# Stick-breaking heads taken two at a time, and five small pads in SBUF

## The chip, the cores and the metric

One NeuronCore of a Trainium2 chip runs the whole program. The metric is the device time of one execution in microseconds. Of the kernel before, three executions took 3411.0, 3412.67 and 3414.54 us; a fourth was taken with the hardware profiler.

## The reference, cut to what matters

The reference is a chain of three transformer-like blocks on 512 tokens of 1024 channels in float32: an HGRN2 mixer, a Mamba-2 mixer and two convolutional feed-forwards; then a block with two attentions side by side; then a third block with latent attention, a convolution and a SwiGLU feed-forward. The part that the change rewrites is the stick-breaking attention of the second block, 8 heads of 64 channels:

```python
def stick_breaking_attention(q, k, v):
    # A[t,s] = beta[t,s] * prod_{s<j<t}(1-beta[t,j]), s<t
    z = einsum('bhqd,bshd->bhqs', qblk, k) * scale
    causal = kpos[None, :] < qpos[:, None]
    log_beta = log_sigmoid(z)
    log_1mb = where(causal, log_sigmoid(-z), 0.0)
    suffix = cumsum(log_1mb, axis=3, reverse=True) - log_1mb
    a = where(causal, exp(log_beta + suffix), 0.0)
    return einsum('bhqs,bshd->bqhd', a, v)
```

Beside it runs a sliding-window attention of 8 heads. Both results go through projections of their own (`w_up_a` for the stick heads, `w_up_b` for the window heads), are gated, summed and projected by `w_o`.

## The kernel before, in words

**Dense products.** Nearly all of the work is x times a weight matrix. Every float32 operand is split into a rounded part and a rest, both of type float32r (`split`, line 241: ScalarE copies the rounded part, VectorE subtracts). One block of 128 by 128 weights times 512 tokens is then three matmuls, lines 188 to 190 in `accumulate`: high weight by high x, high weight by low x, low weight by high x. The weights are the stationary operand and are split in the pool `wp` (tiles `whi`, `wlo`, three buffers each, line 165 on); the moving operand is a tile of 128 partitions by 512 float32, 2048 bytes in each partition. The x of a projection (`xh`, `xl`) lies in the pool `res`. Other moving operands lie in pools of the stage: `hh`, `hl` (hidden units of four feed-forwards, in pools `ffn`, `ffn`, `ffr` and `swi`), `ogh`, `ogl` in `hg`, `yh`, `yl` in `mb`, `oah`, `oal`, `obh`, `obl` in `at_c`, `mh`, `ml` in `at_g`, and in the third block `qah`, `kvh`, `krh`, `ph`, `at` and `mg` in its `t3` pools and `pe`.

**Where a tile lies.** Pools lie in SBUF one behind the other in the order in which they are opened, and the tiles of a pool in the order of their first use. `const`, `res`, `wp` and `tp` are opened once, in this order (lines 99 to 102); every pool of a stage lies behind `tp`. `hg` lies behind the small pool `hg_c`, `mb` behind `mb_c`, `swi` behind `xout`, and `t3_x`, `pe`, `t3_q` and `t3_h` behind `t3_k`, while `t3_g` lies where `t3_k` was, once that is closed.

**The attention stage** (`attention2`, line 1116). Its 29 projection products (`v0 v1 q0 k0 g g w1 ...`, line 1186 on) stand in a list `fill`, and the loop of line 1207 writes the program in turns: in each turn every live attention head does one step, and one projection product is taken from the list. One window head is live at a time (four steps, `window_steps`), and up to two stick heads, started at least three turns apart (`gap`, line 1221). A stick head (`stick_steps`, line 1349) does six steps: for query block i = 3, 2, 1, 0 the scores q.k of (i + 1) * 128 keys (line 1368), two sigmoids on ScalarE, two triangular selects on GpSimd, the transposes of the block before (line 1359) with their copies, and on VectorE a reversed product scan (line 1382) and a product (line 1386); then the last transposes; then the product with v (line 1393). The head's 64 channels lie in partitions 0 to 63 or 64 to 127, so line 1368 contracts over 64 rows, half of TensorE's array, and line 1393 makes 64 columns, the other kind of half. Both have plain float32 operands, and each such matmul runs as two passes. After the loop come `gated(w_up_b, ob)` and `gated(w_up_a, oa)`, lines 1253 and 1254, 96 matmuls each.

**What sets the order.** The program's order is a priority: the framework that builds the kernel orders the instructions of each engine ahead of time, and takes a later instruction earlier where its operands are ready. On the chip each engine then goes through its list in order. Worked through by hand, the loop of line 1207 takes 32 turns, with a product from `fill` in turns 0 to 27.

The start of a head in the loop, and the scores and the product with v of a head:

```python
if sticks and n < 2 and ("k", 0) in have and (n == 0 or tick >= gap):
    h = sticks.pop(0)
    while ("k", h // 2) not in have:
        fill.pop()()
...
    nc.tensor.matmul(ps[:, :w], q[:, i * P : w], k[:, :w], start=True, stop=True)
...
    nc.tensor.matmul(
        po[dst, j * P :], va[j][:, 64 * h : 64 * h + 64], at[:, at0[j] : at0[j] + NT - j * P], start=j == 0, stop=j == 3,
    )
```

Of the kernel before, what the change touches and what calls it, by code (L numbers as in the profile page):

```python
# [8 lines left out]
F32 = mybir.dt.float32  # L9
# [3 lines left out]
AF = mybir.ActivationFunctionType  # L13
ALU = mybir.AluOpType
AX = mybir.AxisListType
PSUM = bass.MemoryType.PSUM
P = 128
# [18 lines left out]
def flat_rows(ap):  # L36
    names = "abcd"[: len(ap.shape)]
    f = ap.rearrange(f"{' '.join(names)} -> ({' '.join(names)})") if len(ap.shape) > 1 else ap
    return f.rearrange("(r c) -> r c", c=P)


def view(t, off, dims):

    return bass.AP(t.tensor, t.offset + off, [t.ap[0], *dims])
# [49 lines left out]
class Net:  # L94
    def __init__(self, ctx, tc, ins):
        self.ctx, self.tc, self.nc, self.I = ctx, tc, tc.nc, ins
        self.n = 0
        pool = lambda name, bufs, **kw: ctx.enter_context(tc.tile_pool(name=name, bufs=bufs, **kw))
        self.const = pool("const", 1)
        self.res = pool("res", 1)  # L100
        self.wp = pool("wp", 2)
        self.tp = pool("tp", 2)
        self.mm = pool("mm", 4, space=PSUM)
        self.aux = pool("aux", 4, space=PSUM)
        nc = self.nc
        self.ident = self.const.tile([P, P], F32, tag="ident", name="ident")
        make_identity(nc, self.ident)
        self.ones = self.const.tile([P, P], F32, tag="ones", name="ones")
        nc.gpsimd.memset(self.ones, 1.0)
        self.zero = self.const.tile([P, 1], F32, tag="zero", name="zero")  # L110
        nc.gpsimd.memset(self.zero, 0.0)
        self.mhalf = self.const.tile([P, 16], F32, tag="mhalf", name="mhalf")
        nc.gpsimd.memset(self.mhalf, -0.5)
        self.xT = [self.res.tile([P, NT], F32, tag=f"x{j}", name=f"x{j}") for j in range(DT)]
        self.xh = self.xl = None
        self.early = []
        self.rows = self.load_rows()
# [335 lines left out]
    def hgrn2(self, nxt):  # L453
# [4 lines left out]
        with ExitStack() as st:  # L458
            pool = lambda name, bufs: st.enter_context(tc.tile_pool(name=name, bufs=bufs, reuse_waits="tile"))
            hc, hp = pool("hg_c", 1), pool("hg", 2)  # L460
            masks = hc.tile([P, 8, P], U8, tag="masks", name="hg_masks")
            for half in range(2):
                mf = self.tmp("t", bufs=5)
# [231 lines left out]
    def mamba(self, nxt):  # L695
# [6 lines left out]
        with ExitStack() as st:  # L702
            pool = lambda name, bufs, **kw: st.enter_context(tc.tile_pool(name=name, bufs=bufs, **kw))
            mc, mp = pool("mb_c", 1), pool("mb", 2)
            dram = pool("mb_d", 1, space=bass.MemoryType.DRAM)


# [408 lines left out]
    def attention2(self, nxt):  # L1116
# [5 lines left out]
        with ExitStack() as st:  # L1122
# [8 lines left out]
            with ExitStack() as st2:  # L1131
# [69 lines left out]
                fill = fill[::-1]  # L1201
                do_wq(0)
                wins = [(i, e) for i in range(4) for e in range(2)]
                sticks = list(range(8))
                live = {}
                tick = 0
                while wins or sticks or live:
                    if wins and not any(n[0] == "w" for n in live):
# [2 lines left out]
                            fill.pop()()  # L1211
                        hs = slice(64 * e, 64 * e + 64)
                        live["w", i, e] = self.window_steps(wp_, have["wq", i][hs], kb[hs], vb, e, sink, ob, 4 * e + i)
                    n = sum(n[0] == "s" for n in live)
                    if sticks and n < 2 and ("k", 0) in have and (n == 0 or tick >= gap):
                        h = sticks.pop(0)
                        while ("k", h // 2) not in have:
                            fill.pop()()
                        hs = slice(64 * (h % 2), 64 * (h % 2) + 64)
                        live["s", h] = self.stick_steps(sp, have["q", h // 2][hs], have["k", h // 2][hs], va, h, oa)  # L1220
                        gap = tick + 3
                    for name in list(live):
                        if next(live[name], "end") == "end":
                            del live[name]
# [121 lines left out]
        hi, lo = ob[h // 2]  # L1346
        self.split(hi[dst], lo[dst], po[dst])

    def stick_steps(self, pool, q, k, va, h, oa):

        nc = self.nc
        dst = slice(64 * (h % 2), 64 * (h % 2) + 64)
        at = pool.tile([P, 10 * P], F32, tag="sat", name=self.nm("sat"), bufs=2)
        at0 = [0, 4 * P, 7 * P, 9 * P]

        def turn(be, i):
            ps = self.psum("aux")
            for j in range(i + 1):
                nc.tensor.transpose(ps[:, j * P : (j + 1) * P], be[:, j * P : (j + 1) * P], self.ident)
            for j in range(i + 1):  # L1360
                to = at0[j] + (i - j) * P
                nc.scalar.activation(at[:, to : to + P], ps[:, j * P : (j + 1) * P], AF.Copy)

        last = None
        for i in (3, 2, 1, 0):
            w = (i + 1) * P
            ps = self.psum("aux")
            nc.tensor.matmul(ps[:, :w], q[:, i * P : w], k[:, :w], start=True, stop=True)  # L1368
            be = pool.tile([P, NT], F32, tag="be", name=self.nm("be"), bufs=3)
            om = pool.tile([P, NT], F32, tag="om", name=self.nm("om"), bufs=2)  # L1370
            nc.scalar.activation(om[:, :w], ps[:, :w], AF.Sigmoid, scale=-1.0)
            nc.scalar.activation(be[:, :w], ps[:, :w], AF.Sigmoid)
            for t, to in ((om, 1.0), (be, 0.0)):
                nc.gpsimd.affine_select(
                    out=t[:, i * P : w], in_=t[:, i * P : w], pattern=[[-1, P]], compare_op=ALU.is_gt, fill=to,
                    base=0, channel_multiplier=1,
                )
            if last:
                turn(*last)
            sc = pool.tile([P, NT], F32, tag="sc", name=self.nm("sc"), bufs=1)  # L1380
            nc.vector.memset(sc[:, w - 1 : w], 1.0)
            nc.vector.tensor_tensor_scan(
                out=view(sc, w - 2, [(-1, w - 1)]), data0=view(om, w - 1, [(-1, w - 1)]),
                data1=view(self.zero, 0, [(0, w - 1)]), initial=1.0, op0=ALU.mult, op1=ALU.add,
            )
            nc.vector.tensor_tensor(out=be[:, :w], in0=be[:, :w], in1=sc[:, :w], op=ALU.mult)
            last = (be, i)
            yield
        turn(*last)
        yield  # L1390
        po = self.psum("aux")
        for j in range(4):
            nc.tensor.matmul(
                po[dst, j * P :], va[j][:, 64 * h : 64 * h + 64], at[:, at0[j] : at0[j] + NT - j * P], start=j == 0, stop=j == 3,
            )
        hi, lo = oa[h // 2]
        self.split(hi[dst], lo[dst], po[dst])

    def relu_ffn(self, nxt, beside):

# [219 lines left out]
    def third(self, before):  # L1620
# [7 lines left out]
        with ExitStack() as st:  # L1628
# [9 lines left out]
            with ExitStack() as s2:  # L1638
# [7 lines left out]
                kr = tuple(kp.tile([P, NK], F32R, tag=f"kr{x}", name=f"kr{x}") for x in "hl")  # L1646
                rk = kp.tile([P, NK], F32, tag="rk", name="rk")
                rkc = kp.tile([P, 6], F32, tag="rkc", name="rkc")
                sqk = rk

                def latent(dst, ps, n, at, gain, sq, first):
# [368 lines left out]
    def swiglu(self, dst):  # L2020
# [6 lines left out]
        with ExitStack() as st:  # L2027
            pool = lambda name, bufs: st.enter_context(self.tc.tile_pool(name=name, bufs=bufs, reuse_waits="tile"))
            xp, fp = pool("xout", 1), pool("swi", 2)
            xo = [xp.tile([P, D], F32, tag=f"xo{c}", name=f"xo{c}") for c in range(4)]  # L2030

            NP = 2
# [143 lines left out]
```

## Time and profile before

| | us |
|---|---|
| median of three executions | 3412.67 |
| the profiled execution, its own time | 3415.03 |
| its span, first to last instruction | 3413.3 |
| TensorE matmul busy (PE) | 3342.7, 98% |
| TensorE weight load busy (PEld) | 2755.6, 81% |
| VectorE busy (DVE) | 2254.0, 66% |
| ScalarE busy (ACT) | 1464.2, 43% |
| GpSimd busy (POOL) | 69.2, 2% |

The profiled execution is 2.36 us over the median, and 1.7 us of it lie outside the span. Matmuls are pipelined: a 128x512 one is shown as some 0.39 us long, while the next one starts after 0.23 us. So the cost of a stream of matmuls is read from the starts, not from the durations.

### The profile page before, as it was taken

The numbers are of one execution on the slowest core, as the hardware profiler recorded it, in microseconds if no ns is written. First come the engines' busy times: TensorE is split into PE (matmuls) and PEld (weight loads), VectorE is DVE, ScalarE is ACT, GpSimd is POOL, SyncE is SP. The second block draws the span as 40 slices with busy tenths as digits, with TensorE's granted clock in tenths as the row PEclk, the third lists the DMA queues.
The fourth block names the chain that finished last, engine by engine and source line by source line (L and its number), as shares of the span: only waits on it lengthen the run. The fifth ranks groups of instructions, "written<-read, shape, count | busy, mean of one in ns | idle before, by whom it ended". The sixth has DMA issues, their size and how long they took to land.

```text
span 3413.3 us, 42607 instructions
## 1 busy us (share of the span) xinstructions
PE 3342.7 (98%) x16365; PEld 2755.6 (81%) x16365; DVE 2254.0 (66%) x3509; ACT 1464.2 (43%) x2505; POOL 69.2 (2%) x110
## 2 busy tenths in 40 slices
PE   8999999997999999999999999999999999999998
PEld 6888788886888887888877778888778888888887
DVE  5777756467888777465655587664669889654334
ACT  4344433234655554232455533333546666332223
POOL 0000000000000000000001100000000000000000
PEclk9999999998999999999999999999999999999999
DMA  4222233233444432333332265552333223423232
GB/s 118 79 63 62 63 99 97 95 93 78 129 117 117 133 112 81 99 94 98 92 87 78 89 193 172 177 170 93 100 87 87 85 76 106 139 87 99 94 98 74
DMA packets 409962, 350.43 MB, mean 103 GB/s; under 512 B 33704, under 2 KB 373407, under 8 KB 409759
## 3 DMA queue, kind: packets, MB, share of 16 engines
q1 hardware_dynamic: 405173, 345.42, 33.3%
q8 instruction: 129, 2.11, 0.3%
q10 hardware_dynamic: 4586, 2.29, 0.2%
q14 instruction: 74, 0.61, 0.1%
HBM read 333.75 MB, written 12.86 MB: 102 GB/s over the span
## 4 chain that ended last, share of the span: by engine, by line
PE 81%; DVE 3%; ACT 1%; DMA 1%; issue 1%; POOL 0%; SPq 0%; ACTq 0%; POOLq 0%; DVEq 0%
PE mm L188 23%; PE mm L190 22%; PE mm L189 22%; PE aux L1043 2%; PE aux L1980 2%; PE aux L2013 1%; PE aux L315 1%; PE aux L1368 1%; PE aux L2004 1%; PE aux L1010 1%; PE mm L1595 1%; PE aux L1065 1%; PE mm L1596 1%; PE mm L1597 1%; DVE wlo L243 1%
## 5 line engine op out<-in xcount | busy, mean ns | idle before, releaser
L188 PE MATMUL mm<-xh,whi 128*128 128x512 f32 x2584 | 1024.5, 396 | 3.4 <-ACT whi L242 2.0
L189 PE MATMUL mm<-xl,whi 128*128 128x512 f32 x2584 | 1013.4, 392 | 6.8 <-DVE xl L243 4.9
L190 PE MATMUL mm<-xh,wlo 128*128 128x512 f32 x2584 | 1011.9, 392 | 6.4 <-DVE wlo L243 6.3
L242 ACT ACTIVATE whi<-raw 128x1024 fp32r<-128x1024 f32 (+3 forms) x532 | 541.9, 1020 | 1087.0 <-PE mm L189 834.8
L243 DVE TENSOR_TENSOR wlo<-raw,whi 128x1024 fp32r<-128x1024 f32 (+3 forms) x532 | 625.1, 1176 | 509.4 <-ACT whi L242 501.1
L188 PEld LDWEIGHTS mm<-xh,whi 128*128 128x128 f32 x2584 | 487.3, 189 | 115.5 <-issue 12.3
L190 PEld LDWEIGHTS mm<-xh,wlo 128*128 128x128 f32 x2584 | 486.9, 188 | 111.3 <-DVE wlo L243 8.8
L189 PEld LDWEIGHTS mm<-xl,whi 128*128 128x128 f32 x2584 | 487.3, 189 | 108.0 <-DVE xl L243 5.2
L188 PE MATMUL mm<-hh,whi 128*128 128x512 f32 x784 | 309.5, 395 | 0.0
L190 PE MATMUL mm<-hh,wlo 128*128 128x512 f32 x784 | 308.7, 394 | 0.0
L189 PE MATMUL mm<-hl,whi 128*128 128x512 f32 x784 | 308.0, 393 | 0.0
L1916 DVE SCALAR_TENSOR_TENSOR cv<-cu,taps,cv 128x511 f32<-128x511 f32 (+14 forms) x240 | 178.1, 742 | 4.4 <-ACT cv L1912 0.7
L190 PEld LDWEIGHTS mm<-hh,wlo 128*128 128x128 f32 x784 | 146.8, 187 | 35.7
L189 PEld LDWEIGHTS mm<-hl,whi 128*128 128x128 f32 x784 | 146.8, 187 | 35.1
L188 PEld LDWEIGHTS mm<-hh,whi 128*128 128x128 f32 x784 | 146.9, 187 | 34.5
L393 DVE TENSOR_TENSOR x<-x,mm 128x512 f32<-128x512 f32 x136 | 93.1, 686 | 99.3 <-PE mm L190 99.2
L960 ACT ACTIVATE w<-w,mb_cum 128x128 f32<-128x128 f32 x256 | 80.9, 393 | 73.0 <-DMA w<-mb_rows 66.6
L242 ACT ACTIVATE hh<-t 128x512 fp32r<-128x512 f32 x98 | 61.4, 627 | 87.3 <-DVE t L430 57.5
L243 DVE TENSOR_TENSOR hl<-t,hh 128x512 fp32r<-128x512 f32 x98 | 67.6, 690 | 42.0 <-ACT hh L242 41.8
L737 DVE SCALAR_TENSOR_TENSOR cy<-mm,cols,cy 128x510 f32<-128x510 f32 (+1 forms) x112 | 83.4, 746 | 2.2 <-ACT cy L733 1.6
L1509 DVE SCALAR_TENSOR_TENSOR acc<-wm,silu_c,acc 128x512 f32<-128x512 f32 x112 | 81.1, 750 | 4.7 <-DMA wm<-in_w_mod_dram 3.3
L1043 PEld LDWEIGHTS aux<-w,xd 128*64 128x64 f32 x512 | 54.9, 137 | 12.2 <-issue 5.3
(517 smaller groups left out, 4672.5 us busy)
## 6 DMA issues: line engine op xcount, KB each, us to landing
raw<-in_ffn_w_in_dram SPq DMA_DIRECT2D x88, 512.0 KB
raw<-in_w_in_dram SPq DMA_DIRECT2D x69, 512.0 KB
raw<-in_w_ff_dram SPq DMA_DIRECT2D x64, 512.0 KB
raw<-in_w_dram SPq DMA_DIRECT2D x64, 512.0 KB
raw<-in_b_w_in_dram SPq DMA_DIRECT2D x48, 512.0 KB
wm<-in_w_mod_dram SPq DMA_DIRECT2D x48, 512.0 KB
raw<-in_a_w_in_dram SPq DMA_DIRECT2D x40, 512.0 KB
raw<-in_ffn_w_out_dram SPq DMA_DIRECT2D x40, 512.0 KB
```

The source lines that it names most:

```text
L188: nc.tensor.matmul(ps, hi[:, k, ms], xh, start=a + k == 0, stop=False)
L189: nc.tensor.matmul(ps, hi[:, k, ms], xl, start=False, stop=False)
L190: nc.tensor.matmul(ps, lo[:, k, ms], xh, start=False, stop=a + k == len(xs) - 1)
L242: self.nc.scalar.activation(hi, src, AF.Copy)
L243: self.nc.vector.tensor_tensor(out=lo, in0=src, in1=hi.bitcast(F32), op=ALU.subtract)
L393: self.nc.vector.tensor_tensor(out=self.xT[j], in0=self.xT[j], in1=ps, op=ALU.add)
L737: nc.vector.scalar_tensor_tensor(out=y[:, to], in0=src[:, at], scalar=cw(tap, j), in1=y[:, to], op0=ALU.mult, op1=ALU.add)
L960: nc.scalar.activation(w[:, d, c, :], w[:, d, c, :], AF.Relu, scale=-1.0, bias=dec["cum"][:, c, h : h + 1])
L1043: nc.tensor.matmul(py[64 * hh : 64 * hh + 64, cs[c]], xd[c][:, d, hd, :], w[:, d, c, :], start=d == 0, stop=d == 1)
L1509: nc.vector.scalar_tensor_tensor(out=ac, in0=t[:, kk], scalar=col, in1=ac, op0=ALU.mult, op1=ALU.add)
L1916: nc.vector.scalar_tensor_tensor(out=y[:, dst], in0=u[:, src], scalar=taps[:, 15 + o : 16 + o], in1=y[:, dst], op0=ALU.mult, op1=ALU.add)
L1980: nc.tensor.matmul(ps[:, :n], a, b, start=i == 0, stop=i == 4)
```

## The change

Two edits. `pad` reserves some bytes in a pool and nothing ever touches them: 320 bytes per partition in `tp`, 320 in `hg_c`, 192 in `mb_c`, 448 in `t3_k` (behind its large tiles) and 384 in `xout`. With them the first byte of every split operand lies at 448 modulo 512 in its partition. And `stick_steps` takes a pair of heads: both halves of the 128 partitions, each matmul of one head right beside that of the other; the scan gets a step of its own, so that a pair has ten steps in place of a head's six; one pair is live at a time; `be` gets a fourth buffer; the result of both heads is split at once. Worked through by hand, the loop then takes 44 turns, with a product from `fill` in turns 0 to 28.

```diff
--- before.py
+++ after.py
@@ -39,6 +39,12 @@
     return f.rearrange("(r c) -> r c", c=P)
 
 
+def pad(pool, name, nbytes):
+
+
+    pool.tile([P, nbytes // 4], F32, tag="pad", name=f"pad_{name}", bufs=1)
+
+
 def view(t, off, dims):
 
     return bass.AP(t.tensor, t.offset + off, [t.ap[0], *dims])
@@ -102,6 +108,7 @@
         self.tp = pool("tp", 2)
         self.mm = pool("mm", 4, space=PSUM)
         self.aux = pool("aux", 4, space=PSUM)
+        pad(self.tp, "tp", 320)
         nc = self.nc
         self.ident = self.const.tile([P, P], F32, tag="ident", name="ident")
         make_identity(nc, self.ident)
@@ -458,6 +465,7 @@
         with ExitStack() as st:
             pool = lambda name, bufs: st.enter_context(tc.tile_pool(name=name, bufs=bufs, reuse_waits="tile"))
             hc, hp = pool("hg_c", 1), pool("hg", 2)
+            pad(hc, "hg", 320)
             masks = hc.tile([P, 8, P], U8, tag="masks", name="hg_masks")
             for half in range(2):
                 mf = self.tmp("t", bufs=5)
@@ -702,6 +710,7 @@
         with ExitStack() as st:
             pool = lambda name, bufs, **kw: st.enter_context(tc.tile_pool(name=name, bufs=bufs, **kw))
             mc, mp = pool("mb_c", 1), pool("mb", 2)
+            pad(mc, "mb", 192)
             dram = pool("mb_d", 1, space=bass.MemoryType.DRAM)
 
 
@@ -1201,7 +1210,7 @@
                 fill = fill[::-1]
                 do_wq(0)
                 wins = [(i, e) for i in range(4) for e in range(2)]
-                sticks = list(range(8))
+                sticks = list(range(4))
                 live = {}
                 tick = 0
                 while wins or sticks or live:
@@ -1211,14 +1220,11 @@
                             fill.pop()()
                         hs = slice(64 * e, 64 * e + 64)
                         live["w", i, e] = self.window_steps(wp_, have["wq", i][hs], kb[hs], vb, e, sink, ob, 4 * e + i)
-                    n = sum(n[0] == "s" for n in live)
-                    if sticks and n < 2 and ("k", 0) in have and (n == 0 or tick >= gap):
-                        h = sticks.pop(0)
-                        while ("k", h // 2) not in have:
+                    if sticks and ("k", 0) in have and not any(n[0] == "s" for n in live):
+                        p = sticks.pop(0)
+                        while ("k", p) not in have:
                             fill.pop()()
-                        hs = slice(64 * (h % 2), 64 * (h % 2) + 64)
-                        live["s", h] = self.stick_steps(sp, have["q", h // 2][hs], have["k", h // 2][hs], va, h, oa)
-                        gap = tick + 3
+                        live["s", p] = self.stick_steps(sp, have["q", p], have["k", p], va, p, oa)
                     for name in list(live):
                         if next(live[name], "end") == "end":
                             del live[name]
@@ -1346,55 +1352,63 @@
         hi, lo = ob[h // 2]
         self.split(hi[dst], lo[dst], po[dst])
 
-    def stick_steps(self, pool, q, k, va, h, oa):
...
+    def stick_steps(self, pool, q, k, va, p, oa):
+
+
+
+        nc = self.nc
+        half = [slice(64 * e, 64 * e + 64) for e in range(2)]
+        at = [pool.tile([P, 10 * P], F32, tag="sat", name=self.nm("sat"), bufs=2) for e in range(2)]
         at0 = [0, 4 * P, 7 * P, 9 * P]
 
+        def turn(bes, i):
+            for e, be in enumerate(bes):
+                ps = self.psum("aux")
+                for j in range(i + 1):
+                    nc.tensor.transpose(ps[:, j * P : (j + 1) * P], be[:, j * P : (j + 1) * P], self.ident)
+                for j in range(i + 1):
+                    to = at0[j] + (i - j) * P
+                    nc.scalar.activation(at[e][:, to : to + P], ps[:, j * P : (j + 1) * P], AF.Copy)
 
         last = None
         for i in (3, 2, 1, 0):
             w = (i + 1) * P
+            pss = [self.psum("aux") for e in range(2)]
+            for e, hs in enumerate(half):
+                nc.tensor.matmul(pss[e][:, :w], q[hs, i * P : w], k[hs, :w], start=True, stop=True)
+            bes = [pool.tile([P, NT], F32, tag="be", name=self.nm("be"), bufs=4) for e in range(2)]
+            oms = [pool.tile([P, NT], F32, tag="om", name=self.nm("om"), bufs=2) for e in range(2)]
+            for om, be, ps in zip(oms, bes, pss):
+                nc.scalar.activation(om[:, :w], ps[:, :w], AF.Sigmoid, scale=-1.0)
+                nc.scalar.activation(be[:, :w], ps[:, :w], AF.Sigmoid)
+                for t, to in ((om, 1.0), (be, 0.0)):
+                    nc.gpsimd.affine_select(
+                        out=t[:, i * P : w], in_=t[:, i * P : w], pattern=[[-1, P]], compare_op=ALU.is_gt, fill=to,
+                        base=0, channel_multiplier=1,
+                    )
             if last:
                 turn(*last)
+            yield
+            for om, be in zip(oms, bes):
+                sc = pool.tile([P, NT], F32, tag="sc", name=self.nm("sc"), bufs=1)
+                nc.vector.memset(sc[:, w - 1 : w], 1.0)
+                nc.vector.tensor_tensor_scan(
+                    out=view(sc, w - 2, [(-1, w - 1)]), data0=view(om, w - 1, [(-1, w - 1)]),
+                    data1=view(self.zero, 0, [(0, w - 1)]), initial=1.0, op0=ALU.mult, op1=ALU.add,
+                )
+                nc.vector.tensor_tensor(out=be[:, :w], in0=be[:, :w], in1=sc[:, :w], op=ALU.mult)
+            last = (bes, i)
             yield
         turn(*last)
         yield
         po = self.psum("aux")
         for j in range(4):
+            for e, hs in enumerate(half):
+                nc.tensor.matmul(
+                    po[hs, j * P :], va[j][:, 128 * p + 64 * e : 128 * p + 64 * e + 64],
+                    at[e][:, at0[j] : at0[j] + NT - j * P], start=j == 0, stop=j == 3,
+                )
+        self.split(*oa[p], po)
 
...
@@ -1646,6 +1660,7 @@
                 kr = tuple(kp.tile([P, NK], F32R, tag=f"kr{x}", name=f"kr{x}") for x in "hl")
                 rk = kp.tile([P, NK], F32, tag="rk", name="rk")
                 rkc = kp.tile([P, 6], F32, tag="rkc", name="rkc")
+                pad(kp, "t3", 448)
                 sqk = rk
 
                 def latent(dst, ps, n, at, gain, sq, first):
@@ -2027,6 +2042,7 @@
         with ExitStack() as st:
             pool = lambda name, bufs: st.enter_context(self.tc.tile_pool(name=name, bufs=bufs, reuse_waits="tile"))
             xp, fp = pool("xout", 1), pool("swi", 2)
+            pad(xp, "xout", 384)
             xo = [xp.tile([P, D], F32, tag=f"xo{c}", name=f"xo{c}") for c in range(4)]
 
             NP = 2
```

## Rows read from the trace of the kernel before

**Rows 1.** The page: engines and TensorE's clock in 40 slices; the chain that ended last.

```profile
PE 3342.7 (98%) x16365; PEld 2755.6 (81%) x16365; DVE 2254.0 (66%) x3509; ACT 1464.2 (43%) x2505; POOL 69.2 (2%) x110
...
PEclk9999999998999999999999999999999999999999
...
PE 81%; DVE 3%; ACT 1%; DMA 1%; issue 1%; POOL 0%; SPq 0%; ACTq 0%; POOLq 0%; DVEq 0%
```

**Rows 2.** Busy time by stretch: us, then PE, PEld, DVE, ACT, POOL, each with count.

```profile
493.49:538.05 44.56, 44.56 (x192) 35.72 (x191) 15.93 (x17) 9.00 (x9) 0.00 (x0) 1.00 0.30 95
538.29:625.12 86.83, 86.83 (x384) 71.91 (x383) 55.82 (x71) 31.29 (x39) 0.00 (x0) 1.00 0.30 97
...
2369.05:2413.61 44.56, 44.56 (x192) 35.72 (x191) 23.68 (x31) 17.67 (x24) 0.00 (x0) 1.00 0.25 83
...
3124.11:3167.84 43.73, 43.73 (x192) 35.87 (x191) 16.36 (x17) 9.01 (x9) 0.00 (x0) 1.00 0.30 96
...
2005.26:2049.83 44.57, 44.57 (x192) 35.91 (x191) 43.75 (x63) 17.88 (x24) 0.00 (x0) 1.00 0.64 204
```

**Rows 3.** The costliest groups of TensorE, shapes apart: the products with hidden units.

```profile
L188 PE MATMUL mm<-hh,whi 128*128 128x512 f32 x784 | 309.5, 395 | 0.0
```

**Rows 4.** TensorE in order of time: scores of 384 keys, of 128 keys.

```profile
1744.29 0.39 PE L190 MATMUL mm<-xh,wlo 128*128 128x512 f32 x1
1744.60 0.91 PE L1368 MATMUL aux<-k,q 64*128 64x384 f32 x2
1745.44 0.66 PE L1359 MATMUL aux<-ident,be 128*128 128x128 f32 x4
...
1951.46 0.48 PE L1368 MATMUL aux<-k,q 64*128 64x128 f32 x2
1951.88 0.44 PE L1359 MATMUL aux<-ident,be 128*128 128x128 f32 x2
```

**Rows 5.** TensorE in order of time: one head's product with v.

```profile
1776.65 0.39 PE L190 MATMUL mm<-xh,wlo 128*128 128x512 f32 x1
1776.97 2.37 PE L1393 MATMUL aux<-sat,va 128*64 128x512 f32 x8
1779.27 0.70 PE L1368 MATMUL aux<-k,q 64*128 64x256 f32 x2
```

**Rows 6.** TensorE in order of time: two heads in different halves of the array.

```profile
1737.87 0.69 PE L1368 MATMUL aux<-k,q 64*128 64x512 f32 x1
1737.99 0.59 PE L1296 MATMUL aux<-kb,wq 64*128 64x256 f32 x2
1738.40 0.59 PE L1368 MATMUL aux<-k,q 64*128 64x512 f32 x1
1738.42 0.38 PE L1296 MATMUL aux<-kb,wq 64*128 64x256 f32 x1
...
1943.19 0.43 PE L1343 MATMUL aux<-wpt,vb 128*64 128x128 f32 x2
1943.40 0.38 PE L1393 MATMUL aux<-sat,va 128*64 128x256 f32 x1
1943.46 0.38 PE L1343 MATMUL aux<-wpt,vb 128*64 128x128 f32 x2
1943.62 0.27 PE L1393 MATMUL aux<-sat,va 128*64 128x128 f32 x1
```

**Rows 7.** Busy time by stretch: the attention loop from the first stick head on.

```profile
1737.00:1953.90 216.90, 216.71 (x982) 156.33 (x981) 124.29 (x231) 120.86 (x281) 29.57 (x64) 1.00 0.28 82
```

**Rows 8.** TensorE in order of time: the end of the loop.

```profile
1953.96 0.50 PE L188 MATMUL mm<-obh,whi 128*128 128x512 f32 x1
...
1955.67 2.37 PE L1393 MATMUL aux<-sat,va 128*64 128x512 f32 x8
...
1968.76 0.73 PE L188 MATMUL mm<-obh,whi 128*128 128x512 f32 x2 [0.68 <-ACT obh L242]
```

**Rows 9.** The scan and the product of the stick heads: ns, min, median, max.

```profile
L1382 DVE TENSOR_TENSOR_SCAN sc<-om,zero x32: 404/864/1223, 1741.7 to 1953.9; 128x511 f32<-128x511 f32 x8, 128x383 f32<-128x383 f32 x8, 128x255 f32<-128x255 f32 x8, 128x127 f32<-128x127 f32 x8
...
L1386 DVE TENSOR_TENSOR be<-be,sc x32: 291/489/693, 1743.0 to 1954.5; 128x512 f32<-128x512 f32 x8, 128x384 f32<-128x384 f32 x8, 128x256 f32<-128x256 f32 x8, 128x128 f32<-128x128 f32 x8
```

More of the change, by code (lines that the diff above doesn't have):

```diff
@@ L1347, in window_steps @@
         self.split(hi[dst], lo[dst], po[dst])
-    def stick_steps(self, pool, q, k, va, h, oa):
+    def stick_steps(self, pool, q, k, va, p, oa):
         nc = self.nc
-        dst = slice(64 * (h % 2), 64 * (h % 2) + 64)
-        at = pool.tile([P, 10 * P], F32, tag="sat", name=self.nm("sat"), bufs=2)
+        half = [slice(64 * e, 64 * e + 64) for e in range(2)]
+        at = [pool.tile([P, 10 * P], F32, tag="sat", name=self.nm("sat"), bufs=2) for e in range(2)]
         at0 = [0, 4 * P, 7 * P, 9 * P]
[L1356 to L1362, printed above, removed]
+        def turn(bes, i):
[6 more added lines that the diff above has]
+                    nc.scalar.activation(at[e][:, to : to + P], ps[:, j * P : (j + 1) * P], AF.Copy)
         last = None
@@ L1366, in stick_steps @@
             w = (i + 1) * P
[L1367 to L1377, printed above, removed]
+            pss = [self.psum("aux") for e in range(2)]
@@ L1378, in stick_steps @@
             if last:
                 turn(*last)
[L1380 to L1386, printed above, removed]
@@ L1387, in stick_steps @@
-            last = (be, i)
+            yield
[7 more added lines that the diff above has]
+                nc.vector.tensor_tensor(out=be[:, :w], in0=be[:, :w], in1=sc[:, :w], op=ALU.mult)
@@ L1392, in stick_steps @@
         for j in range(4):
[L1393 to L1397, printed above, removed]
+            for e, hs in enumerate(half):
[4 more added lines that the diff above has]
+        self.split(*oa[p], po)
     def relu_ffn(self, nxt, beside):
```

## The prediction, made before the changed kernel ran

> **What bounds the kernel now.** I read the page first. TensorE is busy 98% of the span at a granted clock that is full in every slice but one, and the chain that ended last runs 81% of the span over TensorE [rows 1]; VectorE, the next, stands at 66%. So time is won where TensorE's stream gets shorter, and lost where something makes it wait. Durations don't tell how fast the stream runs, starts do: I took stretches that hold one kind of product only, from the first start to the last, and divided by the count less one [rows 2].
>
> There the stretches part. With `xh`, `xl` as the moving operand 384 matmuls start in 86.83 us, one per 226.7 ns. With `hh`, `hl` of the feed-forward 192 take 44.56 us, 233.3 ns, and the same in `ffr`; in `swi` 43.73 us, 229.0 ns; with `mh`, `ml` 44.57 us, 233.4 ns. Same shape, same weights pool, clock 1.00 in each row. What differs is the place of the moving operand. By the change every split operand ends up at 448 modulo 512; less the pads that lie ahead of it that gives its place now. `res` and `wp` lie ahead of all pads: 448 already. Behind `tp` alone (feed-forwards, `at_c`, `at_g`, `t3_k`, `t3_g`): 448 - 320 = 128. `hg`: 448 - 640 = 320. `mb`: 448 - 512, that is 448 already (its 192 only repairs what the pad in `tp` would do). `t3_q`, `t3_h`, `t3_x`, `pe`: 192. `swi`: 256. So 448 goes with 226.7 ns, 128 with 233.3, 256 with 229.0.
>
> **Term 1, the pads.** They add no instruction. Each 512-column matmul that moves from 128 to 448 should gain 233.3 - 226.7 = 6.6 ns, from 256 it gains 2.3. Hidden units: 784 of each kind [rows 3], 2352 in all; `swi` has 22 * 8 * 3 = 528 of them, the others 1824. 1824 * 6.6 = 12.0 us and 528 * 2.3 = 1.2. In attention `oa`, `ob` and `mh` make 384 matmuls, 2.5 us; in the third block `at` and `mg` make 384, 2.5 us. Some 550 more lie at 320, 192, or in `t3_k`, in stretches mixed with other work, where I have no clean row: between 0 and 6.6 ns each, 0 to 3.6 us; I take the middle of the two nearest rows, some 4 ns, 2.0 us. Sum 20.2 us, bounds 18.2 and 21.8. All of it is on the path, since TensorE has no idle time in these stretches. VectorE is at 98% of the stretch with `mh` [rows 2], but with the modulation's own work, which runs on after it.
>
> **Term 2, the pairs.** Now: scores of 384 keys take 0.84 us from their first start to the next instruction's, those of 128 keys 0.42 [rows 4]; so 128 keys more cost 0.21 and 0.21 is a fixed part; 256 and 512 keys come to 0.63 and 1.05. The matmul ahead of them is followed after 0.31 instead of 0.23, so 0.08 more per visit. A head's four scores: 2.94 + 0.33 = 3.27 us. Its product with v: 2.30, and 0.09 ahead of it [rows 5], 2.39. Eight heads: 45.3 us.
>
> In pairs the same number of passes run, but in two halves of the array. Whether these run at once the trace of before shows by chance [rows 6]. Scores of a window head in rows 64 to 127 (L1296) go on at 0.43 us for two 256-column passes while a stick head's scores (L1368) run in rows 0 to 63; and a window head's products (L1343) start at 1943.19 in one half of the columns while L1393 goes on in the other, 0.22 us for a 256-column pass, the 0.21 that it costs alone. So a pair should cost one head and a lag, in which the second head's weights are loaded: between 0 and the fixed 0.21 per score; I take 0.2, and half of it for the product with v, whose weights have 64 columns. A pair: 3.27 + 0.8 + 2.39 + 0.1 = 6.6 us, four 26.2, saved 19.1. Bounds: no lag, 22.7; nothing at once, only visits shared, 16 * 0.29 + 4 * 0.24 = 5.6.
>
> The Trainium skill, page "TensorE: Matmul & The Clock Gate", section "Part 3: Packing small matmuls — row/col tiling", says that matmuls are strict FIFO in start and end, with no reordering. As the program has both passes of one head ahead of those of the other, by that rule only the second pass of one would run beside the first of the other: 14.8 us saved instead of 19.1. Rows 6 speak against it: passes of one half start between queued passes of the other, each at its own pace.
>
> **What else moves.** Four splits fewer on ScalarE and VectorE, a fourth `be` buffer, the scan in a step of its own: nothing, since from the first stick head to the end of the loop TensorE is busy 216.71 of 216.90 us and VectorE 57%, ScalarE 56% [rows 7]; TensorE's projection products cover them. That cover is what the change takes: a pair has ten steps and only one is live, so turns 29 to 43 have no projection product left, and the second half of pair 2 and all of pair 3 are written there. Pair 3's own chain: VectorE 2 * 4 * (0.864 + 0.489) = 10.8 us [rows 9], some 2 us ahead of it for scores, sigmoid and select, and behind it 4.2 us from the last scores at 1951.46 [rows 4] to the product with v at 1955.67 [rows 8] and 2.5 for that: 19 us, with the half pair 28. To cover it TensorE has 96 matmuls of `w_up_b`, 22 us, which need window heads alone, 10 us of the pairs' own work, some 3 us of the last window head, and the first blocks of `w_up_a`: 35 us and more. The kernel before already takes such products ahead: `obh` starts at 1953.96, before the last L1393, and waits 0.68 us once [rows 8]. I charge 1.5 us for waits like that; it could be none or 5.
>
> **Sum.** Against the profiled execution: 3415.03 - 20.2 - 19.1 + 1.5 = 3377.2 us. That execution is 2.36 us over the median of the runs, so 3374.9, say **3375 us**.
>
> **Rivals.**
> - *Halves in strict order*: a pass starts only when all passes written ahead of it have started, and those of its own half have ended. Then of four passes of scores three stay in line: a pair saves one pass in each block, 2.1 / 2 = 1.05 us, and a visit, 4 * 0.19, in sum 1.8 us; of its products with v (0.43, 0.32, 0.21 and 0.11 us a pass) 2.58 us stay in line, with 0.34 for the visit 2.9 instead of 4.8. Four pairs save 14.8 us: 3379. Against it: rows 6, in both kinds of halves. For it: there the two heads' passes were not written alternately. It is the rule of the Trainium skill that is named above. Chance 0.17.
> - *No overlap* in pairs, as both moving operands come through one path: 5.6 saved, 3388. Rows 6 show full pace with small operands only (128 and 256 columns). Chance 0.06.
> - *The pads do nothing*, because a tile that nothing touches gets no bytes, or because the pitch goes with the pool's use and not with the address. Against it: `swi` and the feed-forwards run the same code and differ only in place, 229.0 against 233.3. Then 3395. Chance 0.08.
> - *The bare end of the loop, slower.* Place: turns 29 to 43. If the order built for TensorE leaves the `w_up_b` products behind the last pair, TensorE idles for the chain less the pairs' own 10 us: 28 - 10 = 18 us, still a gain in sum. It turns into a loss where the chain goes over some 48 us, since 38 are won elsewhere; at twice the 28, as weight splits and windows share VectorE and ScalarE, 46 us idle: 3421 us, and more if TensorE's clock falls in the gap. Rows 8 speak against the first half of this. Chance 0.05.
>
> **How the numbers follow.** The forecast has the rest, 0.64. The range reaches from both terms at their upper bounds without a wait (3412.7 - 21.8 - 22.7 = 3368, and 2 us for the runs' own spread) over the strict order to no overlap, 3388 and 2: 3366 to 3390. It leaves out the pads' failure and the slower case, 0.13, and some of what I don't see. A measurement of this kernel can tell about 0.2%, 6.8 us, from no change: faster by more 0.93, within it 0.02, slower 0.05.
>
> **What would show it.** Right: `hh` stretches of 192 matmuls in 43.3 us instead of 44.56; L1368's successor with one visit of two heads per query block, some 1.35 us for 512 keys; no idle time of TensorE over 2 us behind the last projection product. Wrong: `hh` still at 233 ns; a pair's product with v over 4 us; a wait of TensorE for a copy, a scan or `oa` in the last turns, with a clock under 1.00 behind it.

## The result, and the profile after

| | before | after |
|---|---|---|
| median, us | 3413.57 (4 runs, 3411.0 to 3414.54) | 3384.94 (4 runs, 3381.95 to 3387.61) |
| span of the profiled execution, us | 3413.3 | 3384.5 |

The ratio is 0.9915, interval [0.9903, 0.9927]: 28.6 us faster, where 38 were forecast. The sign and the range hold; 10 us of the gain are missing. In the changed kernel lines 195 to 197 are the three products of a block (188 to 190 before), 249 and 250 the split, 1368 the transposes, 1378 the scores, 1399 the product behind the scan, 1407 the product with v, 1247 the evacuation `mg` of the `w_up_b` products.

The page, engines' busy time:

```profile
PE 3309.8 (98%) x16365; PEld 2752.1 (81%) x16365; DVE 2248.7 (66%) x3505; ACT 1456.0 (43%) x2497; POOL 71.5 (2%) x110
```

TensorE has the same number of instructions as in [rows 1] and 32.9 us less busy time. Busy time by stretch, columns as in [rows 2]: `hh` of the first feed-forward, `xh` and `xl`, then `hh` of `ffr` and `swi`, and `mh`:

```profile
491.79:535.08 43.29, 43.29 (x192) 35.85 (x191) 15.92 (x17) 9.01 (x9) 0.00 (x0) 1.00 0.31 98
535.31:622.12 86.81, 86.81 (x384) 71.88 (x383) 55.83 (x71) 31.30 (x39) 0.00 (x0) 1.00 0.31 97
2345.30:2388.59 43.29, 43.29 (x192) 35.85 (x191) 23.52 (x31) 17.69 (x24) 0.00 (x0) 1.00 0.26 85
3096.62:3139.91 43.29, 43.29 (x192) 35.85 (x191) 16.35 (x17) 9.01 (x9) 0.00 (x0) 1.00 0.31 97
1986.65:2029.95 43.30, 43.30 (x193) 35.85 (x192) 43.06 (x63) 18.12 (x24) 0.00 (x0) 1.00 0.67 212
```

All run at 43.29 / 191 = 226.7 ns now, as `xh` did. TensorE in order of time: scores of 384 keys of a pair; then the third pair's product with v and the last pair's scores of 512 and 384 keys:

```profile
1743.15 0.92 PE L1378 MATMUL aux<-k,q 64*128 64x384 f32 x4
1744.00 0.66 PE L1368 MATMUL aux<-ident,be 128*128 128x128 f32 x4
...
1925.86 2.37 PE L1407 MATMUL aux<-sat,va 128*64 128x512 f32 x16
1928.16 2.40 PE L1378 MATMUL aux<-k,q 64*128 64x512 f32 x8
1930.50 0.51 PE L196 MATMUL mm<-obl,whi 128*128 128x512 f32 x1
1932.47 0.66 PE L1368 MATMUL aux<-ident,be 128*128 128x128 f32 x4 [1.47 <-DVE be L1399]
```

Sixteen passes take 2.30 us from their first start to the next instruction's, what eight took in [rows 5], and a pair's scores of 384 keys take 0.85 us, where one head's took 0.84 [rows 4]: the two heads run side by side. So both edits do what the prediction said; the last line shows where time is lost. Busy time by stretch, from the first scores to the first product with `mh`: the whole, then the part up to the third pair's product with v, then the end in pieces:

```profile
1729.56:1986.65 257.09, 251.34 (x1200) 191.15 (x1199) 150.87 (x276) 129.98 (x303) 32.08 (x64) 0.98 0.34 103
1729.56:1925.86 196.30, 195.51 (x961) 150.45 (x960) 112.46 (x216) 107.89 (x251) 22.68 (x48) 1.00 0.32 93
1925.86:1932.47 6.61, 5.14 (x26) 2.22 (x26) 2.68 (x4) 3.50 (x7) 2.29 (x4) 1.00 0.17 61
1932.47:1937.00 4.53, 4.53 (x18) 2.81 (x19) 4.24 (x8) 3.47 (x13) 2.91 (x5) 0.62 0.01 2
1937.00:1948.30 11.30, 10.56 (x54) 6.46 (x52) 6.37 (x16) 5.12 (x22) 4.21 (x8) 1.00 0.41 141
1948.30:1951.06 2.76, 0.00 (x1) 0.01 (x1) 1.88 (x3) 0.84 (x1) 0.00 (x0) 0.86 0.00 0
1951.06:1957.00 5.94, 5.94 (x14) 4.70 (x15) 2.15 (x4) 0.00 (x0) 0.00 (x0) 0.50 0.78 265
1957.00:1986.65 29.65, 29.65 (x131) 24.50 (x131) 21.09 (x29) 9.16 (x12) 0.00 (x0) 1.00 0.51 159
```

What to see: two idle stretches of TensorE, 1.47 and 2.76 us. Behind the first the granted clock is 0.62 on average over 4.53 us, behind the second 0.50 over 5.94 us; 0.50 is the lower level, 1.2 GHz, and 0.62 a mean of both levels. In the 5.94 us only 14 products start; at 226.7 ns that takes 3.17. The three largest waits of TensorE in the whole stretch, us in total, times, longest:

```profile
PE mm L195 <- DVE mg L1247: 2.8, 1, 2.8
PE aux L1368 <- DVE be L1399: 1.5, 1, 1.5
PE aux L1368 <- ACT om L1382: 0.4, 1, 0.4
```

This stretch took 267.39 us before, from 1737.87 to 2005.26, with 266.17 of them busy. It is the measure below, since whole runs of one kernel differ by some 5 us.

### The profile page after: what moved, and what is told of

It is laid out like the page before. It is cut to its first block, busy times and chain, and to the rows that moved or that the text cites. A ratio compares the mean times of both kernels' runs of the same rounds, so it can differ in the third digit from the quotient of the medians.

```text
span 3384.5 us, 42574 instructions
## 1 busy us (share of the span) xinstructions
PE 3309.8 (98%) x16365; PEld 2752.1 (81%) x16365; DVE 2248.7 (66%) x3505; ACT 1456.0 (43%) x2497; POOL 71.5 (2%) x110
## 4 chain that ended last, share of the span: by engine, by line
PE 81%; DVE 3%; ACT 1%; DMA 1%; issue 1%; POOL 1%; SPq 0%; ACTq 0%; POOLq 0%; DVEq 0%
PE mm L195 22%; PE mm L197 22%; PE mm L196 22%; PE aux L1052 2%; PE aux L1995 2%; PE aux L2028 1%; PE aux L322 1%; PE aux L1019 1%; PE aux L2019 1%; PE aux L1074 1%; PE mm L1609 1%; PE mm L1610 1%; PE mm L1611 1%; DVE wlo L250 0%; POOL rsq_y L311 0%
## 5 line engine op out<-in xcount | busy, mean ns | idle before, releaser
L1052 PEld LDWEIGHTS aux<-w,xd 128*64 128x64 f32 x512 | 54.9, 137 | 12.2 <-issue 5.0
```

The source lines that it names most:

```text
L1052: nc.tensor.matmul(py[64 * hh : 64 * hh + 64, cs[c]], xd[c][:, d, hd, :], w[:, d, c, :], start=d == 0, stop=d == 1)
```

## The experiments

**The two edits apart.** `e1_pads` is the kernel before with the five pads; `e2_pairs` the changed kernel without them. The times of `e3_places`, `e4_places`, `e5_weights` and of `e8_places` to `e11_last_free` are of a single execution each, so it is their stretches that count.

> The kernel before with the five pads alone, heads one by one as before. Theory (the pads gave all that was forecast, the pairs half of it): 20 us under the kernel before, some 3393.5 us; the end of the attention loop has no idle time of TensorE over 1 us, as before. Rival (the pairs gave their 19 us, and the pads only the other 9 or 10): some 3404 us.

> The changed kernel without its five pads. Theory: the pairs save 17 to 19 us of TensorE's time and give back 8 to 9 us in the last turns of the loop, in two idle stretches of TensorE of 1 to 3 us each and some 6 to 8 us at half its clock behind them: 9 us under the kernel before, some 3404.5 us, and the idle stretches stand there without pads too. Rival (the pads made the bad end of the loop, by other addresses): no idle stretch over 1 us, 17 to 19 us saved, some 3395 us.

Pads alone: 3397.52 us against 3415.36 of before in the same session, ratio 0.9944, interval [0.9928, 0.9961], 17.8 us. Pairs alone: 3403.18 against 3415.36, 0.9965, [0.9952, 0.9978], 12.2 us. Together they make 30.0, the changed kernel 28.6: within the noise the edits add up. `e1_pads` is nearer to its theory (3393.5) than to its rival (3404). The attention stretch:

```profile
1729.63:1995.70 266.07, 264.85 (x1201) 194.86 (x1199) 155.86 (x280) 137.04 (x310) 29.76 (x64) 1.00 0.34 100
```

(`e1_pads`) and

```profile
1736.91:1993.26 256.35, 250.48 (x1201) 189.90 (x1199) 151.05 (x276) 130.43 (x303) 31.91 (x64) 0.99 0.34 104
```

(`e2_pairs`). The pads take 1.3 us from it, the pairs 11.0 without pads and 266.07 - 257.09 = 9.0 with them; part of the 2 us between the two is TensorE's clock, on average 0.99 in `e2_pairs` and 0.98 in the changed kernel. The wait of 2.8 us for `mg` and that of 1.5 us for `be` stand in `e2_pairs` too, so the theory holds and its rival falls.

**The place of an operand.** `e3_places`, `e4_places` and `e8_places` put other pads into the pools of the four feed-forwards of the changed kernel; `e3_places` for instance

```diff
         with self.tc.tile_pool(name=self.nm("ffn"), bufs=2) as fp:
+            self.nffn = getattr(self, "nffn", 0) + 1
+            shift = (64, 128)[self.nffn - 1]
+            if shift:
+                pad(fp, self.nm("ffn"), shift)
...
+            pad(fp, "ffr", 256)
...
-            pad(xp, "xout", 384)
+            pad(xp, "xout", 256)
```

> The changed kernel with the hidden units moved: first convolutional feed-forward at 0 modulo 512, second at 64, the relu feed-forward at 192, the last at 320. Theory (the place modulo 512 sets the pace of a 512-column product, whatever the pool): four different paces, each the same all through its stage, between 226 and 234 ns, and 226.7 where nothing moved; I expect 192 and 320 between the two that are known, about 231 and 228 ns, and 0 and 64 unknown, 227 to 235. Rival (any pad mends it, or the pace belongs to the pool): 226.7 ns everywhere. In sum 0 to 12 us slower than the changed kernel.

> The same with other places: first feed-forward at 384, second at 480, the relu feed-forward at 416, the last at 128. Theory: the last, which runs at 229.0 ns at 256 and at 226.7 at 448, goes to 233.3 ns at 128, as the other pools did; 384, 416 and 480 come close to 448, 226 to 229 ns. Rival (the pace belongs to the pool): 226.7 ns everywhere, or the last at 229.0 again. In sum 3 to 7 us slower than the changed kernel.

> The changed kernel with the hidden units at 32 (first feed-forward), 96 (second), 224 (relu) and 288 (last) modulo 512. So far 192 and 448 gave 226.7 ns, 0 and 256 gave 229.0, and 64, 128, 320, 384, 416 and 480 gave 233.3, as if only the place modulo 256 counted. Theory (modulo 256): 224 as 480, 233.3 ns; 288 the same as 32, at one of the three paces; 96 between 64 and 128, 233.3. Rival (modulo 512 or finer): 224 at 226.7 or 229.0, and 32 and 288 differ.

Stretches of 192 products of `e3_places`: at 0, 64, 192 and 320 modulo 512.

```profile
491.25:534.99 43.74, 43.74 (x193) 35.87 (x192) 15.91 (x17) 9.01 (x9) 0.00 (x0) 1.00 0.32 97
1396.20:1440.76 44.56, 44.56 (x192) 35.85 (x191) 15.93 (x17) 9.01 (x9) 0.00 (x0) 1.00 0.30 94
2349.55:2392.84 43.29, 43.29 (x192) 35.85 (x191) 23.51 (x31) 17.68 (x24) 0.00 (x0) 1.00 0.27 85
3100.89:3145.45 44.56, 44.56 (x192) 35.85 (x191) 16.36 (x17) 9.01 (x9) 0.00 (x0) 1.00 0.30 95
```

So 0 gives 229.0 ns, 64 and 320 give 233.3, and 192 gives 226.7, as good as 448; my guesses for 192 and 320 (231 and 228) were wrong. In `e4_places` all four, at 384, 480, 416 and 128, took 44.57 us, 233.3 ns, the near neighbours of 448 too, for which I had expected 226 to 229. `swi`, which had 229.0 ns at 256 [rows 2], goes to 233.3 at 128: the pace is not the pool's. In `e8_places` 32, 288 and 224 gave 44.56 to 44.58 us, 96 gave 44.74. 480 and 128 of `e4_places`, then 32 and 288 of `e8_places`:

```profile
1399.10:1443.67 44.57, 44.57 (x193) 35.80 (x191) 15.91 (x17) 9.02 (x9) 0.00 (x0) 1.00 0.30 94
3113.36:3157.93 44.57, 44.57 (x192) 35.72 (x191) 16.35 (x17) 8.99 (x9) 0.00 (x0) 1.00 0.30 95
...
489.60:534.18 44.58, 44.58 (x193) 35.86 (x191) 15.92 (x17) 9.00 (x9) 0.00 (x0) 1.00 0.30 95
3105.51:3150.09 44.58, 44.58 (x193) 35.86 (x191) 16.35 (x17) 9.00 (x9) 0.00 (x0) 1.00 0.30 95
```

Places 256 bytes apart agree: 32 and 288, 64 and 320, 192 and 448, 128 and 384. So what counts is the place modulo 256, and 32 bytes beside a good place the gain is gone. The runs took 3393.96, 3406.33 and 3398.74 us.

**The place of the weights.** `e5_weights` moves the weights and leaves all moving operands at 448; `e9_both` also moves the hidden units.

```diff
-        pad(self.tp, "tp", 320)
+        pad(self.tp, "tp", 128)
+        pad(self.wp, "wp", 192)
```

> The changed kernel with the weights moved instead: 192 bytes ahead of them put whi and wlo at 128 modulo 512, and the pad in tp is cut to 128, so that all moving operands stay at 448. Theory (it is the place of the moving operand alone): 226.7 ns for all stretches as in the changed kernel, 3385 us. Rival (it is the distance between the moving operand and the weights, or the weights' own place): some 12000 products at another pace, 229 to 233.3 ns, 28 to 80 us slower.

> Weights at 128 modulo 512 (as in the run before, where all products then took 228.9 ns at 448), and the hidden units moved too: first feed-forward at 128, second at 0, relu at 384, last at 128. Theory (the distance from the weights to the moving operand modulo 256 sets the pace: 0 gives 226.7, 64 gives 229, everything else 233.3): 226.7 ns in the first, the relu and the last feed-forward, at places that gave 233.3 with the weights at 448; 233.3 in the second; 228.9 elsewhere. Rival (each operand's own place costs, and the two add up): 6.6 + 2.2 over the floor, some 235.5 ns in the first, the relu and the last, 231.2 in the second.

In `e5_weights`, 3405.51 us, `hh` and `xh` at an unchanged place lose their pace, 43.72 / 191 and 87.67 / 383 = 228.9 ns. The theory (the moving operand's place alone) falls; the run is 20.6 us over the changed kernel, less than the rival's 28 to 80:

```profile
491.06:534.78 43.72, 43.72 (x193) 35.87 (x191) 15.90 (x17) 9.01 (x9) 0.00 (x0) 1.00 0.31 96
535.00:622.67 87.67, 87.67 (x384) 71.93 (x383) 55.83 (x71) 31.38 (x39) 0.00 (x0) 1.00 0.31 96
```

In `e9_both`, 3399.73 us, with the weights still at 128: hidden units at 128, 0, 384, 128, then `mh` at 448:

```profile
489.42:532.74 43.32, 43.32 (x193) 35.86 (x192) 15.90 (x17) 9.01 (x9) 0.00 (x0) 1.00 0.32 97
1397.41:1441.79 44.38, 44.38 (x192) 35.99 (x191) 15.91 (x17) 9.01 (x9) 0.00 (x0) 1.00 0.30 95
2353.97:2397.29 43.32, 43.32 (x192) 35.86 (x191) 23.52 (x31) 17.70 (x24) 0.00 (x0) 1.00 0.27 85
3108.63:3151.94 43.31, 43.31 (x193) 35.85 (x191) 16.35 (x17) 9.01 (x9) 0.00 (x0) 1.00 0.31 97
1992.39:2036.96 44.57, 44.57 (x192) 36.10 (x191) 43.73 (x63) 17.89 (x24) 0.00 (x0) 1.00 0.65 203
```

128 and 384, which gave 233.3 ns with the weights at 448, give 226.8; the rival, which adds up each operand's own cost, falls with them. So it is the distance from the weights to the moving operand: 0 modulo 256 gives the shortest pace, at both places of the weights that were tried. How much another distance costs, 2 to 8 ns, is not as firm: the second line, distance 128, took 232.4 ns where I expected 233.3, and the last, distance 64, 233.3 where `e5_weights` had 228.9 at the same place. That stays open.

**The end of the loop.** `e6_six_steps` takes the separate step of the scan away, `e7_paced` leaves every third turn without a projection product.

```diff
             if last:
                 turn(*last)
-            yield
             for om, be in zip(oms, bes):
```

```diff
-                    if fill:
+                    if fill and tick % 3 != 2:
```

> The changed kernel without the separate step for the scan: a pair has six steps as a head had, and the loop takes 29 turns or so, of which all but one or two have a projection product. Theory (the pairs' lost 8 to 9 us went into idle stretches and a falling clock in turns without products): no wait of TensorE over 1 us in the loop and behind it, clock 1.00, 8 us under the changed kernel, some 3377 us. Rival (the pairs just overlap less than read): 3385 us, the same. A third way: scan and scores in one turn make new waits all over the loop, 3385 us and more.

> The changed kernel, ten steps to a pair as it is, but every third turn takes no product from the list, so that the 29 products last to the end of the loop. Theory (cover): as in the run with six steps, some 3377 us, no wait over 1 us behind the loop. Rival (the separate scan step itself, or less overlap than read, costs the 8 us): 3385 us.

`e6_six_steps`: 3376.25 us, ratio 0.9888, [0.9873, 0.9903]; `e7_paced`: 3380.36, 0.99, [0.9883, 0.9916]. Waits and the attention stretch of `e6_six_steps`:

```profile
PE mm L195 <- ACT obh L249: 0.7, 1, 0.7
...
1728.70:1973.66 244.96, 243.80 (x1201) 187.94 (x1200) 151.81 (x276) 132.90 (x306) 27.94 (x64) 1.00 0.36 108
```

and of `e7_paced`:

```profile
PE aux L1342 <- DVE ws L1334: 1.1, 2, 0.7
PE aux L1368 <- DVE sc L1394: 0.6, 1, 0.6
PE aux L1378 <- ACT be L1383: 0.4, 1, 0.4
...
1728.92:1978.12 249.20, 246.94 (x1192) 187.85 (x1192) 149.39 (x268) 128.03 (x294) 29.82 (x64) 1.00 0.35 106
```

Both have a clock of 1.00 and no wait for `mg`. With cover, ten steps take 257.09 - 249.20 = 7.9 us less than bare, six steps another 4.2. The theory holds, and the rival that blamed the separate scan step falls, since `e7_paced` keeps that step. `e7_paced` came out 3 us slower in the median than expected; its row shows 3.1 us more TensorE time than that of six steps, as the attention's matmuls stand in more and shorter groups between the projection products, and 1.1 us more idle.

**What the 2.8 us wait is.** The pool `mm` has four PSUM buffers, and a block of `w_up_b` is 12 products, four of them with `obl`. In the changed kernel the products with `obl` up to the wait are

```profile
1917.00:1948.30 31.30, 6.80 (x16) 3.14 (x16) 0.69 (x1) 0.95 0.23 77
```

that is four blocks, 48 of the 96 products. All four buffers are full then and wait for `mg`, which stands in VectorE's list behind other work. `e11_last_free` frees it from the last pair, `e12_gates_first` from the weight split.

```diff
-        self.split(*oa[p], po)
+        self.split(*oa[p], self.xT[0] if p == 3 else po)
```

```diff
+        self.hold = []
...
+        if self.hold:
+            nc.vector.tensor_copy(hi[:, :1], self.hold.pop()[:, :1])
         self.split(hi[:, :size], lo[:, :size], raw[:, :size])
...
+            self.hold = [mg[3]]
             gated(I["w_up_a_2"][0], oa, 0, False)
```

> The changed kernel, but the result of the last pair is not used: its split reads a tile of x that has long been there. All else, the ten steps and the bare turns too, as it was. Theory (the 2.8 us wait behind the loop comes from the order of VectorE and ScalarE, where the evacuations of the w_up_b products stand behind the split of the last pair's result): the wait of TensorE for mg falls under 1 us, and the stretch at half clock behind it goes, 3 to 5 us under the changed kernel, some 3381 us. Rival (what they wait for is a weight split, whose buffer TensorE gives free late, or the load of the gates): a wait of 2 us and more stays.

> The changed kernel with one thing added: before the first weights of w_up_a are split, VectorE copies one column of the fourth evacuation of w_up_b into the tile for their high part, so that in the list of VectorE the four evacuations now stand ahead of that split; they still stand behind the split of the last pair's result. Theory (the 2.8 us wait comes from the place of the four evacuations behind a weight split that itself waits for TensorE): the evacuations start some 0.7 us behind the last pair's split of its result, at once as that ends, TensorE waits under 1 us there and its clock stays at 1.00 behind it; 2 to 5 us under the changed kernel, some 3381 us; the earlier idle stretch of 1.5 us, for be, stays. Rival (TensorE then waits for the weights of w_up_a instead, which now come later, or VectorE is late anyway): a wait of 2 us and more stays in the loop's end, 3385 us.

`e11_last_free`, 3384.94 us: my theory fell, and its rival, a weight split, holds. TensorE waits for `mg` as long as ever, and VectorE and ScalarE show for what (start, us, what ended the idle time):

```profile
1948.69 1.06 ACT L249 ACTIVATE whi<-raw 128x1024 fp32r<-128x1024 f32 x1 [4.05 <-PE mm L196]
...
1949.78 1.23 DVE L250 TENSOR_TENSOR wlo<-raw,whi 128x1024 fp32r<-128x1024 f32 x1 [5.89 <-ACT whi L249]
1950.93 2.47 DVE L1247 TENSOR_TENSOR mg<-mm,gl 128x512 f32<-128x512 f32 x4
```

A buffer of `whi` comes free only when TensorE has ended a `w_up_b` product; then come the two halves of the split, then `mg`. In the changed kernel the same three stand at 1948.09, 1949.18 and 1950.32. The theory formed from that put the four `mg` ahead of the split, and in `e12_gates_first` they follow the last pair's split directly:

```profile
1946.63 0.69 DVE L253 TENSOR_TENSOR oal<-aux,oah 128x512 fp32r<-128x512 f32 x1 [3.85 <-ACT oah L252]
1947.23 2.47 DVE L1250 TENSOR_TENSOR mg<-mm,gl 128x512 f32<-128x512 f32 x4
```

Its waits of TensorE, and the stretch behind the place where it had waited:

```profile
PE mm L198 <- DVE mg L1250: 0.2, 1, 0.2
...
1947.77:1950.50 2.73, 2.53 (x11) 2.12 (x12) 2.09 (x5) 0.53 (x1) 0.00 (x0) 1.00 0.45 152
1950.50:1957.00 6.50, 6.50 (x31) 5.37 (x30) 4.28 (x5) 1.60 (x2) 0.00 (x0) 1.00 0.79 248
```

The wait goes from 2.8 to 0.2 us, the clock stays at 1.00 there, and the attention stretch takes 252.53 us, 4.6 less than 257.09. The earlier wait for `be` stays, as expected, and the clock's fall behind that one is longer here, 0.51 on average over 6.53 us. The median, 3381.75 us, ratio 0.99, [0.9883, 0.9916], overlaps that of the changed kernel; the gain is read from the trace.

**The order of passes.** `e10_one_head_first` is the six-step version with the two loops of the product with v exchanged: all passes of one head, then those of the other.

```diff
-        for j in range(4):
-            for e, hs in enumerate(half):
+        for e, hs in enumerate(half):
+            for j in range(4):
```

> The six-step version with the pair's products with v written head by head: all four (eight passes) of the first head, then those of the second. Theory A (the halves of the array go their own way, however the passes are written): the sixteen passes still take 2.3 us, the same time in all. Theory B (passes start in the order in which they are written, and overlap only with the neighbour in that order): some 4.4 us, 8 us more in all. Between them, if TensorE looks only a few passes ahead.

TensorE in order of time:

```profile
1768.37 3.93 PE L1406 MATMUL aux<-sat,va 128*64 128x512 f32 x16
1772.22 0.50 PE L195 MATMUL mm<-xh,whi 128*128 128x512 f32 x1
```

3.85 us against 2.30 in `e6_six_steps`; four pairs make 6.2 us, and the runs differ by 3382.01 - 3376.25 = 5.8. The attention stretch is 251.21 - 244.96 = 6.3 us longer. That lies between A and B. Pass by pass, the first head's eight start at 1768.37, .85, 1769.28, .60, .92, 1770.14, .35 and .46; the second head's first, known by its 512 columns, starts at 1769.93, ahead of three that were written before it. What had started by then, by columns (each head has two passes of 512):

```profile
L1406 PE MATMUL aux<-sat,va x6: 379/539/643, 1768.4 to 1769.9; 128*64 128x512 f32 x3, 128*64 128x384 f32 x2, 128*64 128x256 f32 x1
```

The other three pairs show the same order. So TensorE passed over three waiting passes of the other half, and not over the four that still waited at 1769.60; that each engine goes through its list in order, as said of the kernel before, does not quite hold for TensorE. The Trainium skill, page "TensorE: Matmul & The Clock Gate", section "Part 3: Packing small matmuls — row/col tiling", has matmuls in strict order of start and end, without reordering. This trace does not agree with it for near neighbours; beyond them the written order counts.

## Why the prediction was right, and where it was wrong

By the number alone 3385 lies nearer to the rival "no overlap", 3388, than to the forecast, 3375. That both terms were right is read from the rows.

**Term 1, the pads, 20.2 us: right.** The trace of the changed kernel gives back 1737.87 - 1729.56 = 8.3 us up to the first scores, 1.3 in the attention stretch (`e1_pads`) and, from the first product with `mh` to the end, (3413.3 - 2005.26) - (3384.5 - 1986.65) = 10.2: 19.8 us. The timed difference was 17.8, with an interval of 13 to 25. The rule behind it was incomplete: not the operand's own place modulo 512 but its distance from the weights modulo 256. So operands at 192 had nothing to gain; of the 2.0 us charged for unclear places the 192 products of `hg` at 320 could give 1.3. In the traces the products with `ogh`, `ogl` follow one another after 232 ns (median) before and 227 in `e1_pads`, 0.7 us in all; those with `qah`, `qal`, at 192, gained nothing.

**Term 2, the pairs, 19.1 us: right in mechanism, in size partly by luck.** Summed from each start to the next in the attention stretch, by kind of matmul:

| us | `e1_pads` | after | `e6_six_steps` |
|---|---|---|---|
| scores, both attentions | 33.95 | 24.04 | 22.73 |
| products with v, both | 29.37 | 21.35 | 21.39 |
| transposes | 16.00 | 15.89 | 13.80 |
| projection products, idle time ahead of other work | 186.75 | 195.81 | 187.04 |

Scores and products with v fall by 17.9 us, with six steps by 19.2. The rivals "no overlap" and "strict order" fall with the 2.30 us of a pair; of "strict order" `e10_one_head_first` shows the part that is true. The lag of 0.2 us for each score and 0.1 for a product with v, 3.6 us in all, is not there: 0.85 us for a pair's 384 keys and 2.30 for its product are one head's times. Without a lag the prediction had 22.7. What takes the sum back to 18 or 19 was not worked out; part of it is that a window head already ran beside a stick head before [rows 6], so that this overlap was no gain.

**The charge for waits, 1.5 us, at most 5: this step failed.** The last line of the table grew by 9.1 us: 19.8 + 17.9 - 9.1 = 28.6 us, the measured gain. The prediction named the place (the bare turns), the victims (a wait for a scan's product, a clock under 1.00 behind it) and the cover, `w_up_b` products. It counted that cover in time alone, 35 us of work against a chain of 28. It left out that such a product needs its PSUM buffer evacuated, that VectorE's list had the evacuations behind a weight split, and that the split needs a buffer that TensorE itself must free. So of the 96 products, 22 us, only 48 could run before the first evacuation. The 1.5 us wait for `be` is another one: 22 of the 48 had run by then, and 26 more ran later without an evacuation, but TensorE's list has the transposes ahead of them. Nor did the prediction price the clock, though it named a fall among its signs of being wrong; that sign came true, and the idle time of 2.76 us is over the 2 us that it allowed. Against `e1_pads` the changed kernel has 5.75 - 1.22 = 4.5 us more idle time in the stretch. The two stretches at 0.62 and 0.50 cost, by an estimate from their rows, 4.53 * 0.38 + 5.94 - 3.17 = 4.5 us. Together that is about the 9.1; the match is rough, since some of the clock's cost falls on transposes and scores.

**"Slower" as a bare loop**: its mechanism came true in part; its price, 46 us of idle, did not, with 4.5 us.

**Better than both** is `e6_six_steps`: pairs and pads without the separate scan step, 3376.25 us, close to the 3375 that was forecast for the changed kernel.

## What to carry to other kernels

Where a stage is written in turns that mix a latency chain with covering work, count for every turn whether it still has cover, and check that the cover's results can be evacuated there: cover ends when the PSUM buffers are full. A shorter chain in fewer turns can be worth more than a slack step that looks free. Compare the start-to-start pace of equal matmuls across pools; where it differs, look at the distance between the two operands in SBUF.

## What was not expected of the hardware

With equal shape and clock a 128x512 float32r matmul follows the last after 226.7 or 226.8 ns where weights and moving operand lie a multiple of 256 bytes apart in their partition, and after 228.9 to 234.3 ns at all other distances tried, in steps of 32 bytes; 32 bytes off is enough. Why is open. The granted clock fell behind the 2.76 us idle stretch of the changed kernel (0.50), but behind the same wait in `e11_last_free` it did not:

```profile
1948.88:1951.66 2.78, 0.00 (x1) 0.00 (x0) 1.88 (x3) 0.87 (x1) 0.00 (x0) 1.00 0.00 0
1951.66:1957.00 5.34, 5.34 (x23) 4.43 (x24) 2.43 (x4) 0.00 (x0) 0.00 (x0) 1.00 0.82 290
```

In both the clock had been low before, on average 0.62 from 1932.47 to 1937.00 in the changed kernel and 0.57 from 1932.18 to 1940.13 here. What decides was not tried.
